# Closer steps for the last head pair, later ones for the others, and a first tile that loads x into idle buffers

## Chip, cores and metric

The kernel runs on one core of one Trainium2 chip. The metric is the device time of one execution in microseconds, as the median of several runs.

## The reference

The kernel computes two decoder layers on one sequence of 512 tokens with 1024 features, in float32. What matters here is the attention mixer of the first layer; the rest of the program follows it on the same engines.

```
n    = rms_norm(x, attn_norm)
proj = n @ w_in                                    # 12 heads, all q, k and v at once
qa, ka, va, qb, kb, vb = split(proj)               # q and k are normalized per head
oa = dilated_mixture_attention(qa, ka, va)         # 8 heads: three dilated windows, mixed by their lse
ob = differential_attention(qb, kb, vb)            # 4 heads: softmax(q1 k1) - lam * softmax(q2 k2)
ob = rms_norm(ob, b_sub_norm) * (1 - lam_init)
h  = x + concat(oa, ob) @ w_out
h  = h + conv_ffn(rms_norm(h))                     # then a recurrent mixer and a second conv_ffn
```

## The kernel before

Every matrix is kept as a sum of two halves in the matmul type, hi and lo, and a product is three matmuls: hi times hi, hi times lo, lo times hi. ScalarE (ACT) makes the hi half with a copy, VectorE (DVE) the lo half with a subtraction. That holds for weights (`split`: wh at L110, wl at L112), for x (`x_split`: xh at L237, xl at L239), and for every result that goes into a further product.

The attention stage is a list of steps, `line`, whose order for TensorE (PE) is written out by hand. Its first 128 steps are groups: 8 pairs of heads (n = 0 to 7; pairs 0 to 3 are differential heads, pairs 4 to 7 dilated ones) times 4 weight units u times 4 token blocks b. A group is 6 matmuls with 384 columns. After them come 28 fill groups, `early_out`, of 3 matmuls with 512 columns each: they begin the out projection for four output chunks with the pairs that are done. The last four fill groups use pair 6.

The attention of a pair runs between the groups of the next pairs. `place(g, f)` hangs a function f behind the step at place g; a projection group counts 1, a fill group 0.65. Matmuls and transposes are kept in this order, and other engines are scheduled from the data they need and their place in the program. With end = 16 n + 15, pair n has these functions:

- `qk_square` and `qk_norm`: squares of q and k, and their normalization, on ACT and DVE. `qk_transpose` (qkt, L418): eight transposes, then qh on ACT (L421) and ql on DVE (L423).
- `sc`: scores of rows 0 and 1, then row 2, then row 3 (`products`, two PSUM banks S, L448), each followed by `softmax_row`: maximum on DVE (L459), exp on ACT (L462), reciprocal on DVE (L463). Pairs of dilated heads then scale on ACT (L516), differential heads combine the two maps on DVE (L560).
- `tr`: transposes of one row (L469, PSUM bank pt), copied to pth on ACT (L472) and to ptl on DVE (L473). Row i takes i + 1 transposes. Dilated heads have two such steps per row, s = 0 and 1.
- `out`: the product with v (bank O, L483 to L492). Dilated heads have two, and go on with t (L531, ACT), o (L532, DVE), oh (L535, ACT) and ol (L536, DVE). Differential heads square the result and allocate the bank of its mean, obms.
- `norm` (differential heads): two matmuls for the mean into obms, Ln and Exp on ACT, six DVE operations (L586 to L590, L593).

All these PSUM banks (S, pt, qkt, O, obms) come from one pool of four, `pa`. The projection groups and `early_out` use another pool of four.

The first tile, `first_tile`, loads x and the weights of pair 0 in four units each. Both use the pool `rawp` of four buffers, so the third x unit has to wait until the first buffers are free. Squares of x (L246) and their running sum xacc (L251) stand ahead of the other work of their unit. `token_stats` turns the sum into the scale of each token in group 13 (n = 0, u = 3, b = `TOK` = 1), and the evacuation of pair 0's PSUM banks begins behind it.

At the very end, `down` adds each of the 8 output chunks to the residual (L737) and stores it (L740), from SyncE's queue.

Of the kernel before, what the change touches and what calls it, by code (L numbers as in the profile page):

```python
# [19 lines left out]
P = 128  # L20
# [8 lines left out]

ORDER = (4, 5, 6, 7, 0, 1, 2, 3)  # L30

QK_LAG = 9
AT_LAG = 12
LAST_QK_LAG = 7.5
LAST_AT_LAG = 10

OUT_GROUP = 0.65

BATCHES = ((0, 1), (2,), (3,))

SC_AT = (0, 2, 4)
TR_AT = (6.5, 8.7, 10.9, 13.1)
OUT_AT = 15
NORM_AT = 17
TOK = 1
EARLY = 4
V_BUFS = 3
WARM = 8
# [20 lines left out]
def trunk(  # L69
# [30 lines left out]
    def nm(s):  # L100
        uid[0] += 1
        return f"{s}{uid[0]}"
# [19 lines left out]
    def wunit(ap, n=1024):  # L122
        return split(load(ap, n), n)
# [101 lines left out]
    with ExitStack() as actx:  # L225
# [77 lines left out]

        def first_tile():

            units = []
            for u in range(4):
                ap = w_att[ORDER[0], u]
                if u:
                    xr = load(xT[u])  # L310
                    x_split(xr, (2 * u, 2 * u + 1))
                    units.append(wunit(ap, 2 * CW))
                    with tc.high_priority():
                        x_square(xr, (2 * u, 2 * u + 1))
                    continue
                xr = rawp.tile([P, 2 * S], F32, tag="raw", name=nm("raw"))
                wr = rawp.tile([P, 2 * CW], F32, tag="raw", name=nm("raw"))
                wh = whp.tile([P, 2 * CW], F32R, tag="wh", name=nm("wh"))
                wl = wlp.tile([P, 2 * CW], F32R, tag="wl", name=nm("wl"))
                for j in range(2):  # L320
                    cx, cw = slice(j * S, (j + 1) * S), slice(j * CW, (j + 1) * CW)
                    nc.sync.dma_start(xr[:, cx], xT[u][:, cx])
                    nc.sync.dma_start(wr[:, cw], ap[:, cw])
                    last = x_split(xr, (j,))
                    with tc.issue_after(last.ins):
                        last = A.copy(wh[:, cw], wr[:, cw])
                    V.tensor_tensor(wl[:, cw], wr[:, cw], wh[:, cw].bitcast(F32), ALU.subtract)
                units.append((wh, wl))
                with tc.issue_after(last.ins):
                    x_square(xr, (0, 1))  # L330
            nc.sync.dma_start(pt[:, KC:], par[:, KC:])
            return units

        def group(n, u, b):

            t = tiles[n]
            if b == 0:
                if u == 0:
                    t["banks"] = [mm.tile([P, S], F32, tag="mm", name=nm("pj")) for _ in range(NB)]
                if n == 0:  # L340
                    if u == 0:
                        t["units"] = first_tile()
                    t["w"] = t["units"][u]
                    prefetch(min(u, 2))
                else:
                    t["w"] = next_unit()
            if n == 0 and u == 3 and b == TOK:
                with tc.high_priority():
                    token_stats(x_acc[0])
            wh, wl = t["w"]  # L350
            tb = slice(b * P, (b + 1) * P)
            o = t["banks"][b][:, :CW]
            for j in range(2):
                k = 2 * u + j
                cw = slice(j * CW, (j + 1) * CW)
                pe(T.matmul(o, xs[k][0][:, tb], wh[:, cw], start=k == 0, stop=False))  # L356
                pe(T.matmul(o, xs[k][1][:, tb], wh[:, cw], start=False, stop=False))  # L357
                pe(T.matmul(o, xs[k][0][:, tb], wl[:, cw], start=False, stop=k == KC - 1))  # L358
            if u == 3 and n == 0:
                if b == 0:  # L360
                    t["vraw"] = smp.tile([P, S], F32, tag="t", name=nm("vraw"), bufs=1)
                with tc.high_priority():
                    A.copy(t["vraw"][:, tb], t["banks"][b][:, 2 * P : CW])
            if u == 3 and (n or b >= TOK):
                with tc.high_priority():
                    for e in range(b + 1) if n == 0 and b == TOK else (b,):
                        evacuate(n, e)

        def evacuate(n, b):

            t = tiles[n]
            p = ORDER[n]
# [4 lines left out]
            v4 = t["v"][:, b].rearrange("p (x y e) -> p x y e", x=2, y=2)  # L377
            vh, vl = (v4[:, :, 0], v4[:, :, 1]) if p < 4 else (v4[:, 0], v4[:, 1])
            pj = t["banks"][b]
            A.copy(t["raw"][:, b].rearrange("p i e -> p (i e)"), pj[:, : 2 * P])  # L380
            r = rstd[:, b : b + 1]
            vv = pj[:, 2 * P : 3 * P]
            if n == 0:

                vv = t["vraw"][:, b * P : (b + 1) * P]
            vv = vv.rearrange("p (s e) -> p s e", s=2)
            A.activation(vh, vv, AF.Copy, scale=r)
            setup_mark[0] = V.scalar_tensor_tensor(vl, vv, r, vh.bitcast(F32), ALU.mult, ALU.subtract)

        def qk_square(n, half):  # L390

# [32 lines left out]
                res.append((hi, lo))  # L424

        oT = {}

        def head_bias(h):
            bt = ap2.tile([P, S], F32, tag="bias", name=nm("bias"))
# [74 lines left out]
        def attn_a(n):  # L504

            p = ORDER[n]
            st = {}

            def sc(blocks):
                if blocks[0] == 0:  # L510
                    st["b"] = [head_bias(2 * p + s) for s in range(2)]
                rows = products(tiles[n]["qk"], blocks)
                for i in blocks:
                    for s in range(2):
                        e, r = softmax_row(rows[s, i], i, st["b"][s])
                        A.activation(e, e, AF.Copy, scale=r)  # L516
                        st["e", s, i] = e

            def tr(s, i):
                if i == 0:  # L520
                    st["pt", s] = pt_tiles()
                transposed(st["e", s, i], i, *st["pt", s])

            def out(s):
                ps = bank("O")
                pv(ps, tiles[n]["v"], *st["pt", s], s)
                if s == 0:
# [10 lines left out]
            steps = [(g, partial(sc, b)) for g, b in zip(SC_AT, BATCHES)]  # L538
            steps += [(g + s, partial(tr, s, i)) for i, g in enumerate(TR_AT) for s in range(2)]
            return steps + [(OUT_AT + s, partial(out, s)) for s in range(2)]  # L540

        def attn_b(n):

# [48 lines left out]
                A.copy(hi, o)  # L592
                V.tensor_tensor(lo, o, hi.bitcast(F32), ALU.subtract)  # L593

            steps = [(g, partial(sc, b)) for g, b in zip(SC_AT, BATCHES)]
            steps += [(g, partial(tr, i)) for i, g in enumerate(TR_AT)]
            return steps + [(OUT_AT, out), (NORM_AT, norm)]


        early = []  # L600
# [35 lines left out]
                small_setup()  # L636
                lru.extend(softplus_setup())

        place(16, setup)
        for n in range(NT):  # L640
            last = n == NT - 1
            end = 16 * n + 15
            place(end - 2, partial(urgent, qk_square, n, 0))
            place(end, partial(urgent, qk_square, n, 1))
            place(end + 0.1, partial(urgent, qk_norm, n))
            place(end + (LAST_QK_LAG if last else QK_LAG), partial(qk_transpose, n))
            for g, f in (attn_a if ORDER[n] < 4 else attn_b)(n):
                place(end + (LAST_AT_LAG if last else AT_LAG) + g, f)
        for g in range(max(len(line), max(at) + 1)):
            if g < len(line):  # L650
                line[g]()
# [59 lines left out]
    def ffn(l, nxt, last):  # L711
# [22 lines left out]
        def down(grp, acts):  # L734
            for m in range(KC):
                ps = job(acts)
                V.tensor_tensor(h[m], ps, h[m], ALU.add)  # L737
                if grp == 2:
                    if last:
                        nc.sync.dma_start(outT[m * P : (m + 1) * P, :], h[m])  # L740
                    else:
                        norm_chunk(m, nxt)

        a0 = up(0)
        a1 = up(1)
# [229 lines left out]
```

## Time and profile before

| what | value |
|---|---|
| median of 3 runs | 1200.01 us (1199.91 to 1200.17) |
| profiled execution | 1198.04 us, of which 1196.3 us are the span of the profile |
| PE busy | 1181.7 us, 99% |
| DVE busy | 811.2 us, 68% |
| ACT busy | 585.7 us, 49% |
| granted TensorE clock | 1.0 throughout |
| mean DMA rate | 96 GB/s |

The span runs from the first to the last instruction of the program. PE is busy nearly all the time, so a stretch in which it is not is what a change of order can win. Busy shares hide one thing: matmuls overlap, and a matmul that starts late shows as idle time only from the end of the one before.

### The profile page before, as it was taken

How to read it: one execution, taken by the hardware profiler on the slowest of the kernel's cores; microseconds unless marked ns; L12 is line 12 of the kernel's file. 1: busy time of each engine (PE TensorE's matmuls, PEld its weight loads, DVE VectorE, ACT ScalarE, POOL GpSimd, SP SyncE). 2: the span in 40 equal slices, each digit the busy share in tenths (PEclk: the TensorE clock that was granted, in tenths of full speed). 3: DMA queues.
4: the chain of work that ended last, by engine and by line, in shares of the span. 5: the costliest groups of instructions: out<-in, count | busy, mean ns of one | idle time of the engine just before them, and what ended most of it. 6: DMA issues, size and time to landing. Idle time of an engine off the chain costs nothing.

```text
span 1196.3 us, 14626 instructions
## 1 busy us (share of the span) xinstructions
PE 1181.7 (99%) x5566; PEld 988.7 (83%) x5566; DVE 811.2 (68%) x1326; ACT 585.7 (49%) x951; POOL 0.7 (0%) x6
## 2 busy tenths in 40 slices
PE   9999999899999999999999999999999999999998
PEld 8988888688888888888888878888888888888887
DVE  7878888587777773577446888758777763677431
ACT  7667778665444432344224688444444441444220
POOL 0000000000000000000000000000000000000000
PEclk9999999999999999999999999999999999999999
DMA  8212122063333333332333313322233233323321
GB/s 260 80 62 67 54 67 71 19 199 100 96 98 95 99 94 100 96 99 94 100 94 103 121 36 121 102 95 94 100 93 101 93 101 95 100 92 102 93 84 53
DMA packets 33766, 114.31 MB, mean 96 GB/s; under 512 B 3872, under 2 KB 4384, under 8 KB 33696
## 3 DMA queue, kind: packets, MB, share of 16 engines
q1 hardware_dynamic: 33552, 113.37, 29.7%
q8 instruction: 44, 0.72, 0.2%
q14 instruction: 26, 0.21, 0.1%
q10 hardware_dynamic: 144, 0.00, 0.0%
HBM read 111.27 MB, written 2.10 MB: 95 GB/s over the span
## 4 chain that ended last, share of the span: by engine, by line
PE 83%; ACT 4%; DVE 3%; issue 0%; ACTq 0%
PE mm L126 26%; PE mm L128 26%; PE mm L127 26%; PE pj L356 1%; PE pj L357 1%; PE pj L358 1%; ACT sm L462 1%; PE pt L469 1%; ACT sm L516 0%; ACT wh L110 0%; PE S L448 0%; DVE sm L459 0%; DVE wl L112 0%; DVE u L863 0%; PE O L490 0%
## 5 line engine op out<-in xcount | busy, mean ns | idle before, releaser
L110 ACT CAST wh<-raw 128x1024 fp32r<-128x1024 f32 (+1 forms) x207 | 211.1, 1021 | 291.6 <-PE mm L127 256.9
L128 PE MATMUL mm<-xh,wl 128*128 128x512 f32 x896 | 348.6, 389 | 0.0
L127 PE MATMUL mm<-xl,wh 128*128 128x512 f32 x896 | 348.6, 389 | 0.0
L126 PE MATMUL mm<-xh,wh 128*128 128x512 f32 x896 | 348.6, 389 | 0.0
L112 DVE TENSOR_TENSOR wl<-raw,wh 128x1024 fp32r<-128x1024 f32 (+1 forms) x207 | 244.7, 1183 | 45.6 <-ACT wh L110 42.8
L127 PEld LDWEIGHTS mm<-xl,wh 128*128 128x128 f32 x896 | 168.2, 188 | 35.2
L126 PEld LDWEIGHTS mm<-xh,wh 128*128 128x128 f32 x896 | 168.2, 188 | 35.0
L128 PEld LDWEIGHTS mm<-xh,wl 128*128 128x128 f32 x896 | 168.2, 188 | 34.8
L707 DVE SCALAR_TENSOR_TENSOR cv<-us,pt,cv 128x511 f32<-128x511 f32 (+2 forms) x216 | 160.4, 747 | 3.5
L126 PE MATMUL mm<-fh,wh 128*128 128x512 f32 x384 | 149.4, 389 | 0.0
L127 PE MATMUL mm<-fl,wh 128*128 128x512 f32 x384 | 149.4, 389 | 0.0
L128 PE MATMUL mm<-fh,wl 128*128 128x512 f32 x384 | 149.4, 389 | 0.0
L703 DVE TENSOR_TENSOR us<-mm,rs 128x512 f32<-128x512 f32 x104 | 71.6, 688 | 93.9 <-PE mm L128 93.7
L737 DVE TENSOR_TENSOR h<-mm,h 128x512 f32<-128x512 f32 x48 | 33.2, 691 | 141.4 <-PE mm L128 141.4
L356 PE MATMUL pj<-wh,xh 128*128 128x384 f32 x256 | 91.9, 359 | 0.9 <-ACT wh L110 0.6
L728 ACT CAST fh<-cv 128x512 fp32r<-128x512 f32 x48 | 29.8, 621 | 126.4 <-DVE cv L725 126.4
L358 PE MATMUL pj<-wl,xh 128*128 128x384 f32 x256 | 86.8, 339 | 0.7 <-DVE wl L112 0.7
L357 PE MATMUL pj<-wh,xl 128*128 128x384 f32 x256 | 86.3, 337 | 0.0
L705 ACT ACTIVATE cv<-us,pt 128x512 f32<-128x512 f32 x104 | 84.2, 813 | 0.8 <-DVE us L703 0.6
L126 PEld LDWEIGHTS mm<-fh,wh 128*128 128x128 f32 x384 | 72.1, 188 | 15.1
L127 PEld LDWEIGHTS mm<-fl,wh 128*128 128x128 f32 x384 | 72.1, 188 | 14.9
L128 PEld LDWEIGHTS mm<-fh,wl 128*128 128x128 f32 x384 | 72.1, 188 | 14.9
(202 smaller groups left out, 1234.1 us busy)
## 6 DMA issues: line engine op xcount, KB each, us to landing
raw<-in_w_up_dram SPq DMA_DIRECT2D x96, 512.0 KB, 3.5
raw<-in_w_dn_dram SPq DMA_DIRECT2D x48, 512.0 KB, 3.5
raw<-in_w_att_dram SPq DMA_DIRECT2D x31, 384.0 KB, 3.2
raw<-in_w_ri_dram SPq DMA_DIRECT2D x16, 512.0 KB, 3.5
raw<-in_w_ao_dram SPq DMA_DIRECT2D x8, 512.0 KB, 4.0
raw<-in_w_ro_dram SPq DMA_DIRECT2D x8, 512.0 KB, 3.5
raw<-in_xT_dram SPq DMA_DIRECT2D x7, 512.0 KB, 4.4
out_dram<-h SPq DMA_DIRECT2D x8, 256.0 KB, 2.0
```

Source lines behind the costliest of these rows:

```text
L110: A.copy(hi, src)
L112: V.tensor_tensor(lo, src, hi.bitcast(F32), ALU.subtract)
L126: order(T.matmul(out, wh, xh, start=first, stop=False))
L127: order(T.matmul(out, wh, xl, start=False, stop=False))
L128: return order(T.matmul(out, wl, xh, start=False, stop=last))
L356: pe(T.matmul(o, xs[k][0][:, tb], wh[:, cw], start=k == 0, stop=False))
L357: pe(T.matmul(o, xs[k][1][:, tb], wh[:, cw], start=False, stop=False))
L358: pe(T.matmul(o, xs[k][0][:, tb], wl[:, cw], start=False, stop=k == KC - 1))
L703: V.tensor_tensor(u, ps, state["rs"], ALU.mult)
L705: A.activation(c, u, AF.Identity, scale=col(wcol + (taps - 1) * stride), bias=col(bcol))
L707: V.scalar_tensor_tensor(c[:, d:], u[:, : S - d], col(wcol + (taps - 1 - d) * stride), c[:, d:], ALU.mult, ALU.add)
L737: V.tensor_tensor(h[m], ps, h[m], ALU.add)
```

## The change

The four parts are independent of each other in the code.

- Places. The constants become two tables, `PLACES` for pairs 0 to 6 and `LAST` for pair 7. For pairs 0 to 6, in groups behind the end of the pair: score steps stay at 12, 14 and 16. The transposes of rows 0 and 3 stay in their group, those of rows 1 and 2 go one group later (for the dilated pairs some steps of s = 1 too). The output goes from 27 to 28, where it stands directly ahead of the next pair's first scores, and the normalization from 29 to 30.5, where it stands behind the next pair's second scores. For pair 7 the three score steps, the transposes and the outputs move together: scores behind fill groups 14, 15 and 16 of 28 (counted from 1) instead of 14, 17 and 20; transposes behind 18 to 23 instead of 24 to the end; both outputs behind 24 instead of behind all 28. Pair 6's later steps run among the fill groups as well: its last transposes and its outputs go one or two fill groups later.
- First tile. x goes into the buffers of pth and ptl, which are not used before pair 0's transposes. All ten loads of x and weights are issued at once, then the rest of the parameters. The squares of a unit come behind the splits of the next one, without priority.
- Token statistics go from group 13 to group 17; evacuation of pair 0 no longer waits for them. The scaling of pair 0's v, its `qk_norm` and the small setup (four more loads, L263 to L267) follow there.
- The last output chunk is added in two halves, and each half is stored as soon as it is there, the second one from ACT's queue.

```diff
-QK_LAG = 9
-AT_LAG = 12
-LAST_QK_LAG = 7.5
-LAST_AT_LAG = 10
+BATCHES = ((0, 1), (2,), (3,))
+PLACES = dict(qk=9, sc=(12, 14, 16), tr=(18.9, 21.1, 23.7, 25.8), step=1, out=28, norm=30.5)
+LAST = dict(qk=7.5, sc=(9.8, 10.5, 11.2), tr=(12.7, 13.4, 14.2, 15), step=0.35, out=16.2, norm=18)
 OUT_GROUP = 0.65
-BATCHES = ((0, 1), (2,), (3,))
-SC_AT = (0, 2, 4)
-TR_AT = (6.5, 8.7, 10.9, 13.1)
-OUT_AT = 15
-NORM_AT = 17
-TOK = 1
+TOK = 17
...
         def first_tile():
+            xr = [ap2.tile([P, 13 * P], F32, tag=("pth", "ptl")[u % 2], name=nm("xr"))[:, : 2 * S] for u in range(4)]
+            wr = [rawp.tile([P, 2 * CW], F32, tag="raw", name=nm("raw")) for u in range(4)]
+            for u in range(4):
+                for j in range(2 if u == 0 else 1):
+                    cx, cw = (slice(j * S, (j + 1) * S), slice(j * CW, (j + 1) * CW)) if u == 0 else (slice(None),) * 2
+                    nc.sync.dma_start(xr[u][:, cx], xT[u][:, cx])
+                    nc.sync.dma_start(wr[u][:, cw], w_att[ORDER[0], u][:, cw])
+            nc.sync.dma_start(pt[:, KC:], par[:, KC:])
             units = []
             for u in range(4):
-                ap = w_att[ORDER[0], u]
                 if u:
-                    xr = load(xT[u])
-                    x_split(xr, (2 * u, 2 * u + 1))
-                    units.append(wunit(ap, 2 * CW))
-                    with tc.high_priority():
-                        x_square(xr, (2 * u, 2 * u + 1))
+                    x_split(xr[u], (2 * u, 2 * u + 1))
+                    units.append(split(wr[u], 2 * CW))
+                    x_square(xr[u - 1], (2 * u - 2, 2 * u - 1))
                     continue
...
-                with tc.issue_after(last.ins):
-                    x_square(xr, (0, 1))
-            nc.sync.dma_start(pt[:, KC:], par[:, KC:])
+            x_square(xr[3], (6, 7))
             return units
...
-            if n == 0 and u == 3 and b == TOK:
-                with tc.high_priority():
-                    token_stats(x_acc[0])
...
+        def first_stats():
+            token_stats(x_acc[0])
+            for b in range(NB):
+                scale_v(0, b, tiles[0]["vraw"][:, b * P : (b + 1) * P])
...
+        def where(n):
+            return LAST if n == NT - 1 else PLACES
...
-            steps += [(g + s, partial(tr, s, i)) for i, g in enumerate(TR_AT) for s in range(2)]
-            return steps + [(OUT_AT + s, partial(out, s)) for s in range(2)]
+            steps += [(g + s * at["step"], partial(tr, s, i)) for i, g in enumerate(at["tr"]) for s in range(2)]
+            return steps + [(at["out"] + s * at["step"], partial(out, s)) for s in range(2)]
...
-        place(16, setup)
+        place(TOK, partial(urgent, first_stats))
+        place(TOK + 1, setup)
         for n in range(NT):
-            last = n == NT - 1
             end = 16 * n + 15
             place(end - 2, partial(urgent, qk_square, n, 0))
             place(end, partial(urgent, qk_square, n, 1))
-            place(end + 0.1, partial(urgent, qk_norm, n))
-            place(end + (LAST_QK_LAG if last else QK_LAG), partial(qk_transpose, n))
+            place(end + 0.1 if n else TOK + 0.1, partial(urgent, qk_norm, n))
+            place(end + where(n)["qk"], partial(qk_transpose, n))
...
                 ps = job(acts)
-                V.tensor_tensor(h[m], ps, h[m], ALU.add)
-                if grp == 2:
-                    if last:
-                        nc.sync.dma_start(outT[m * P : (m + 1) * P, :], h[m])
-                    else:
-                        norm_chunk(m, nxt)
+                for t in (slice(0, S // 2), slice(S // 2, S)) if last and grp == 2 and m == KC - 1 else (slice(0, S),):
+                    V.tensor_tensor(h[m][:, t], ps[:, t], h[m][:, t], ALU.add)
+                    if last and grp == 2:
+                        (A if t.start else nc.sync).dma_start(outT[m * P : (m + 1) * P, t], h[m][:, t])
+                if grp == 2 and not last:
+                    norm_chunk(m, nxt)
```

## Rows read from the trace of the kernel before

**Rows 1.** Windows: busy us (instructions) of each engine, clock, DMA share, GB/s.

```profile
60.00:240.00 180.00, 172.77 (x1048) 149.29 (x1047) 138.87 (x398) 132.92 (x342) 0.00 (x0) 1.00 0.18 56
...
240.00:1192.00 952.00, 951.15 (x4191) 785.91 (x4190) 623.02 (x782) 412.10 (x517) 0.00 (x0) 1.00 0.31 98
```

**Rows 2.** Waits of PE, 60 to 246 us: total us, times, longest.

```profile
PE mm L126 <- ACT oh L535: 2.0, 1, 2.0
PE pt L469 <- DVE sm L560: 1.5, 3, 0.5
PE pt L469 <- DVE ptl L473: 1.4, 2, 0.7
PE pt L469 <- DVE mx L459: 1.0, 1, 1.0
PE O L484 <- DVE ptl L473: 0.5, 2, 0.2
PE O L492 <- DVE ptl L473: 0.5, 2, 0.2
PE O L490 <- ACT pth L472: 0.2, 1, 0.2
```

**Rows 3.** Timeline of the first tile: start us, us, instruction, [idle before, releaser].

```profile
8.31 1.34 ACT L237 ACTIVATE xh<-raw,pt 128x512 fp32r<-128x512 f32 x2 [0.65 <-DMA raw<-in_xT_dram]
9.07 1.42 DVE L239 SCALAR_TENSOR_TENSOR xl<-raw,pt,xh 128x512 fp32r<-128x512 f32 x2 [0.69 <-ACT xh L237]
...
10.34 0.33 PE L357 MATMUL pj<-wh,xl 128*128 128x384 f32 x1
...
10.51 0.34 PE L358 MATMUL pj<-wl,xh 128*128 128x384 f32 x1
10.60 0.82 ACT L110 CAST wh<-raw 128x768 fp32r<-128x768 f32 x1
...
11.47 0.44 PE L356 MATMUL pj<-wh,xh 128*128 128x384 f32 x1 [0.62 <-ACT wh L110]
...
11.75 0.34 PE L357 MATMUL pj<-wh,xl 128*128 128x384 f32 x1
11.80 0.95 DVE L112 TENSOR_TENSOR wl<-raw,wh 128x768 fp32r<-128x768 f32 x1
```

**Rows 4.** DMA issues: count, size of each, us from issue to landing.

```profile
out_dram<-h SPq DMA_DIRECT2D x8, 256.0 KB, 2.0
...
pt<-in_par_dram SPq DMA_DIRECT2D x1, 238.5 KB, 6.3
```

**Rows 5.** Timeline of the token statistics and pair 0's normalization, DVE and PE.

```profile
23.89 0.15 DVE L291 TENSOR_SCALAR ssq<-tok 128x4 f32<-128x4 f32 x1
...
31.03 1.28 DVE L409 TENSOR_TENSOR qkraw<-qkraw,rsy 128x512 f32<-128x512 f32 x2
...
35.61 1.03 PE L418 MATMUL qkt<-ident,qkraw 128*128 128x128 f32 x8
```

**Rows 6.** Timeline of pair 3's scores and transposes, PE and DVE.

```profile
122.04 0.50 PE L448 MATMUL S<-qh,qh 64*128 64x512 f32 x2
...
124.39 0.68 DVE L587 SCALAR_TENSOR_TENSOR obt<-obms,obt 128x512 f32<-128x512 f32 x1
...
133.01 0.74 DVE L560 SCALAR_TENSOR_TENSOR sm<-sm,sum,sm 128x512 f32<-128x512 f32 x1
...
134.77 0.60 PE L469 MATMUL pt<-ident,sm 128*128 128x128 f32 x4
```

**Rows 7.** Timeline of ACT in the last pair: first exp, last output.

```profile
216.33 0.40 ACT L462 ACTIVATE sm<-sm,mx 128x128 f32<-128x128 f32 x1 [1.33 <-DVE mx L459]
...
237.16 0.58 ACT L531 COPY t<-O 64x512 f32<-64x512 f32 x1 [0.67 <-PE O L490]
...
238.50 0.62 ACT L535 CAST oh<-o 128x512 fp32r<-128x512 f32 x1 [0.76 <-DVE o L532]
```

**Rows 8.** Window of the last pair, from its first scores to the wait.

```profile
214.90:239.00 24.10, 21.49 (x123) 16.16 (x122) 12.97 (x39) 15.27 (x40) 0.00 (x0) 1.00 0.00 1
```

More of the change, by code (lines that the diff above doesn't have):

```diff
@@ L304, in first_tile @@
         def first_tile():
+            xr = [ap2.tile([P, 13 * P], F32, tag=("pth", "ptl")[u % 2], name=nm("xr"))[:, : 2 * S] for u in range(4)]
[6 more added lines that the diff above has]
+            nc.sync.dma_start(pt[:, KC:], par[:, KC:])
             units = []
             for u in range(4):
-                ap = w_att[ORDER[0], u]
                 if u:
-                    xr = load(xT[u])
-                    x_split(xr, (2 * u, 2 * u + 1))
-                    units.append(wunit(ap, 2 * CW))
-                    with tc.high_priority():
-                        x_square(xr, (2 * u, 2 * u + 1))
+                    x_split(xr[u], (2 * u, 2 * u + 1))
+                    units.append(split(wr[u], 2 * CW))
+                    x_square(xr[u - 1], (2 * u - 2, 2 * u - 1))
                     continue
-                xr = rawp.tile([P, 2 * S], F32, tag="raw", name=nm("raw"))
-                wr = rawp.tile([P, 2 * CW], F32, tag="raw", name=nm("raw"))
                 wh = whp.tile([P, 2 * CW], F32R, tag="wh", name=nm("wh"))
@@ L320, in first_tile @@
                 for j in range(2):
[L321 to L324, printed above, removed]
+                    cw = slice(j * CW, (j + 1) * CW)
+                    last = x_split(xr[0], (j,))
                     with tc.issue_after(last.ins):
-                        last = A.copy(wh[:, cw], wr[:, cw])
-                    V.tensor_tensor(wl[:, cw], wr[:, cw], wh[:, cw].bitcast(F32), ALU.subtract)
+                        A.copy(wh[:, cw], wr[0][:, cw])
+                    V.tensor_tensor(wl[:, cw], wr[0][:, cw], wh[:, cw].bitcast(F32), ALU.subtract)
                 units.append((wh, wl))
-                with tc.issue_after(last.ins):
-                    x_square(xr, (0, 1))
-            nc.sync.dma_start(pt[:, KC:], par[:, KC:])
+            x_square(xr[3], (6, 7))
             return units
@@ L358, in group @@
                 pe(T.matmul(o, xs[k][0][:, tb], wl[:, cw], start=False, stop=k == KC - 1))
-            if u == 3 and n == 0:
-                if b == 0:
-                    t["vraw"] = smp.tile([P, S], F32, tag="t", name=nm("vraw"), bufs=1)
+            if u == 3:
                 with tc.high_priority():
[L363 to L367, printed above, removed]
+                    evacuate(n, b)
+                    if n:
+                        scale_v(n, b, t["banks"][b][:, 2 * P : CW])
         def evacuate(n, b):
             t = tiles[n]
-            p = ORDER[n]
             if b == 0:
@@ L375, in evacuate, with scale_v @@
                 t["v"] = ap2.tile([P, NB, 2 * P], F32R, tag="v", name=nm("v"), bufs=V_BUFS)
-            v4 = t["v"][:, b].rearrange("p (x y e) -> p x y e", x=2, y=2)
-            vh, vl = (v4[:, :, 0], v4[:, :, 1]) if p < 4 else (v4[:, 0], v4[:, 1])
+                if n == 0:
+                    t["vraw"] = smp.tile([P, S], F32, tag="t", name=nm("vraw"), bufs=1)
             pj = t["banks"][b]
             A.copy(t["raw"][:, b].rearrange("p i e -> p (i e)"), pj[:, : 2 * P])
+            if n == 0:
+                A.copy(t["vraw"][:, b * P : (b + 1) * P], pj[:, 2 * P : CW])
+        def scale_v(n, b, v):
+            t = tiles[n]
+            v4 = t["v"][:, b].rearrange("p (x y e) -> p x y e", x=2, y=2)
+            vh, vl = (v4[:, :, 0], v4[:, :, 1]) if ORDER[n] < 4 else (v4[:, 0], v4[:, 1])
             r = rstd[:, b : b + 1]
[L382 to L386, printed above, removed]
+            vv = v.rearrange("p (s e) -> p s e", s=2)
             A.activation(vh, vv, AF.Copy, scale=r)
             setup_mark[0] = V.scalar_tensor_tensor(vl, vv, r, vh.bitcast(F32), ALU.mult, ALU.subtract)
+        def first_stats():
+            token_stats(x_acc[0])
+            for b in range(NB):
+                scale_v(0, b, tiles[0]["vraw"][:, b * P : (b + 1) * P])
         def qk_square(n, half):
@@ L536, in out @@
                     V.tensor_tensor(lo, st["o"], hi.bitcast(F32), ALU.subtract)
-            steps = [(g, partial(sc, b)) for g, b in zip(SC_AT, BATCHES)]
-            steps += [(g + s, partial(tr, s, i)) for i, g in enumerate(TR_AT) for s in range(2)]
-            return steps + [(OUT_AT + s, partial(out, s)) for s in range(2)]
+            at = where(n)
+            steps = [(g, partial(sc, b)) for g, b in zip(at["sc"], BATCHES)]
+            steps += [(g + s * at["step"], partial(tr, s, i)) for i, g in enumerate(at["tr"]) for s in range(2)]
+            return steps + [(at["out"] + s * at["step"], partial(out, s)) for s in range(2)]
         def attn_b(n):
@@ L593, in norm @@
                 V.tensor_tensor(lo, o, hi.bitcast(F32), ALU.subtract)
-            steps = [(g, partial(sc, b)) for g, b in zip(SC_AT, BATCHES)]
-            steps += [(g, partial(tr, i)) for i, g in enumerate(TR_AT)]
-            return steps + [(OUT_AT, out), (NORM_AT, norm)]
+            at = where(n)
+            steps = [(g, partial(sc, b)) for g, b in zip(at["sc"], BATCHES)]
+            steps += [(g, partial(tr, i)) for i, g in enumerate(at["tr"])]
+            return steps + [(at["out"], out), (at["norm"], norm)]
         early = []
@@ L644, in trunk @@
             place(end, partial(urgent, qk_square, n, 1))
-            place(end + 0.1, partial(urgent, qk_norm, n))
-            place(end + (LAST_QK_LAG if last else QK_LAG), partial(qk_transpose, n))
+            place(end + 0.1 if n else TOK + 0.1, partial(urgent, qk_norm, n))
+            place(end + where(n)["qk"], partial(qk_transpose, n))
             for g, f in (attn_a if ORDER[n] < 4 else attn_b)(n):
-                place(end + (LAST_AT_LAG if last else AT_LAG) + g, f)
+                place(end + g, f)
         for g in range(max(len(line), max(at) + 1)):
```

## The prediction

> **What bounds the kernel now.** Read first the windows by stage: from 240 us on TensorE (PE) is busy 951.15 of 952 us, so nothing there can be won but the last store; between 60 and 240 it stands idle 7.2 of 180 us [rows 1]. The change must earn its time in the first 240 us, and it earns it only where PE waits. So read next the waits of PE: after 60 us they are few, and each names the row that came last [rows 2]. Then the timeline at the start, where the second x unit comes late [rows 3].
>
> An idle time reads short. Matmuls overlap: one of 0.33 us is followed by the next after 0.17 us (10.34, 10.51), so an idle of 0.62 us ahead of 11.47 is a distance of 0.96 us where 0.17 is normal, a loss of 0.79 [rows 3]. I add 0.16 us to each idle time below. Three waits on L560 then cost 2.0 us, two on L473 ahead of transposes 1.7, one on L459 1.2, the two at L484 0.8, the two at L492 0.8, the one at L490 0.4, the one on L535 2.2 [rows 2]. With 1.7 us at the start (below) that is about 10.8 us, the most that can come back apart from small change.
>
> **The change part by part.** Durations are from the profiled execution: span 1196.3 us, 1198.04 us with what lies around it. The median of the runs shown is 1200.01 us; I take the same saving off it.
>
> *Start.* Before, PE lost 0.79 us at 11.47, and 0.89 us more until its third matmul: wl ended at 12.75, where 11.47 + 0.28 + 0.17 = 11.92 would have been due, and the handover adds 0.06 [rows 3]. On ScalarE (ACT) two squares stood between xh and wh: xh ends at 9.65, wh could run 0.82 us to 10.47 and PE was free at 10.68. That first wait goes. On VectorE (DVE) the xacc additions stood between xl (ends 10.49) and wl: wl now ends at 10.49 + 0.95 = 11.44, and the third matmul is due at 10.68 + 0.35 = 11.03, so 0.46 us stays. Saving 1.7 - 0.46 = 1.2 us. The x units no longer wait for a weight buffer; that itself is worth little at unit 1, whose x came in the first batch anyhow. Its landing is the unknown: more loads now follow it at once. Before, xh waited 0.65 us for it until 8.31, and the 238.5 KB of parameters that followed took 6.3 us to land, as if they had queued behind the units [rows 3, 4]; if five units instead share the engines evenly, x could come 2 us later. Bounds -0.8 to +1.7. The parameters and the four loads of the small setup go further back on SP's queue; their first reader is the bias of the first scores, after group 27, some 10 us later than any of them should land. POOL has nothing here.
>
> The token statistics move from group 13 to the end of group 17, and the first q/k normalization behind them. Before, 8.4 us passed from the first DVE step at 23.89 to the end of that normalization at 32.31; the transposes that need it came at 35.61 [rows 5]. Group 17 ended seven groups of 1.04 us ahead of those, at 28.3. Now the first step comes at about 28.3 - 1.2 + 0.3 for the handover = 27.4, the transposes at 34.4: 7.0 us. The chain itself is short (small operations, and 1.28 us for the two halves), the 8.4 were mostly other work in between, so I take a wait of 0.3; bounds 0 and 1.5. Behind the waiting transposes stand all projection matmuls. Saving of the start: 0.9.
>
> *Pairs 0 to 6, places.* A group is 6 matmuls, 1.04 us. The third row of pairs 1 to 3 moves one group later, more than the 0.67 us that each waits: 2.0 us back. Their outputs move a group as well: the 0.8 us at L484 goes. Pair 4 lost 0.9 us (of the two L473 waits) and 1.2 us (L459) one behind the other; one group of delay takes 1.04 off the sum: 1.0, bounds 1.0 and 2.1. Output and next scores now follow without a group between, as do scores and normalization: two switches fewer for four pairs; the first matmul after a break hands over after 0.28 us, not 0.17 (11.47, 11.75) [rows 3], 0.1 us for each of eight switches. 0.7, bounds 0 and 1.4.
>
> Against it: the fourth row's place stays in the same group, and PE comes there 0.67 us earlier. In pair 3 its row was ready at 133.01 + 0.74 = 133.75 and PE came at 134.77 [rows 6]: 1.0 us of slack becomes 0.35. The normalization (six DVE operations; if all take the 0.68 us of L587, some 4 us) now falls later into the same DVE burst. Ahead of the row it takes up to 1.2 us, behind it nothing. I take 0.3 us for each of three pairs, 0.9; bounds 0 and 2.6 (three times 1.2 - 0.35). Sum for pairs 0 to 5: 2.0 + 0.8 + 1.0 + 0.7 - 0.9 = 3.6; bounds 1.2 and 6.3.
>
> Pair 6: the second L473 wait (0.8) and one L492 wait (0.4). The transposes move one fill group (0.68 us) later, but so does the second row whose evacuation they wait for: 0.4, bounds -0.3 and 1.2.
>
> *Last pair.* Before, all fill groups were used up when the transposes of the last two rows and both outputs ran; then t, o and oh came one after the other, from 237.16 to 239.12, and PE stood [rows 7]. Now the outputs stand after fill group 24 of 28, and four fill groups (12 matmuls of 512 columns; at 0.17 us for 384 [rows 3] 0.23 us each, 2.7 us) follow: they cover the 2.2 us. That part is firm. The other waits of the stretch (L492 0.4, L490 0.4) add 0.8, so 3.0 us can come back, less the new waits.
>
> New waits: from 214.9 to 239 ACT is busy 15.27 us [rows 8], 1.7 of it t and oh after the outputs, so 13.6 us belong ahead of them. The first exp stood 1.3 us behind the first scores [rows 7], so the last copy ends 14.9 us after them at the earliest, with no gap on ACT, and DVE's half, of the size of L587's 0.68 us [rows 6], 0.7 us later. PE needs 24.1 - 3.4 us of waits (this stretch's and pair 6's L492) - 2.7 fill = 18.0 us to the end of the second output, so the first (2560 columns each, 1.2 us) is due 15.6 us after the first scores; it needs all but the last copy (0.6 like oh [rows 7]), 14.9 - 0.6 + 0.7 = 15.0. ACT may stand 0.6 us, and stood 8.8 of 24.1 us before. I take 1.1 us of new waits, nearer the gapless end, since the scores of all rows now lie ready early; bounds 0 and 3.9 (half of the old idle time stays). Saving 1.9, bounds -0.9 and 3.0.
>
> *Last store.* The 256 KB store takes 2.0 us to landing [rows 4]. Two half additions end a little later than one whole; the second store moves half the bytes and leaves from ACT, which has nothing behind it. Saving 0.2, bounds -0.1 and 0.4. The Trainium skill, page "Perfetto Trace Analysis", section "DMA Optimizations", says that transfers below 2 KB carry much overhead each; the halves have rows of 1 KB. By that the saving would be 0 and the sum 0.2 smaller; no run here shows it.
>
> Sum: 0.9 + 3.6 + 0.4 + 1.9 + 0.2 = 7.0 us: span 1189.3, profiled 1191.0, median 1200.01 - 7.0 = **1193.0 us**.
>
> **Rivals.** *Every wait goes and none comes.* 1.7 + 6.3 + 1.2 + 3.0 + 0.4 = 12.6 us, 1187.4. For it: all delays exceed the waits. Against: ACT gapless for 14 us.
>
> *The waits come back one step later.* In pairs 1 to 4 and the last, ACT and DVE are the late ones (L560, L459, L473) [rows 2]; a later third row only shifts the wait to the fourth row or the output, and the last pair starves. Left: the start, the switches and the store, 0.9 + 0.7 + 0.2 = 1.8 us, 1198.2. For it: fourth rows with 0.35 us left. Against: transposes of row 4 did not wait in pairs 1 to 3. The same Trainium skill page, section "Optimization Strategy", says that a gap repeating on the engine that should be busy can mean too little PSUM for the next tile; by that rule the gap would stay, and this rival's 1198.2 would be the time. The trace agrees for pair 4 (L459 and L473 free a bank), not for pairs 1 to 3, where data (L560) came last.
>
> *Slower: a bank held by the normalization.* Output allocates the bank of the mean, and the normalization now comes behind the next pair's second scores. If the third scores need that bank, they wait for L587: ahead of pair 3 it ended at 125.07 where the scores came at 122.04 [rows 6], 3.0 us, plus 1.2 for the later place: 4.2 us in four pairs, 16.8 - 7.0 = 9.8 slower, 1209.8. It decides from 1.8 us per pair (7.0 / 4). Against: before, too, L587 came after those scores and they did not wait; two other banks served.
>
> **Chances.** Forecast 0.74 (its own range 1188.0 to 1197.0), every wait gone 0.10, waits come back 0.11, slower 0.05. The range 1188.0 to 1198.3 leaves out the first and the last rival. 0.2% is 2.4 us, about what a measurement can tell from no change: faster 0.84, same 0.11, slower 0.05.
>
> **What would show it.** Right: PE's waits on L560 gone; no wait on oh ahead of the out projection; the wait ahead of the second x unit on wl alone, near 0.3 us idle; ACT almost without idle time through the last pair. Wrong: waits at qkt near 35 us, at the fourth row's transposes, at S products, or a late xh at 8.3 us. PE idle between 60 and 240 us should fall from 7.2 to about 2.5 us.

## The result, and the profile after

The changed kernel is slower: 1208.28 us (median of 4 runs, 1206.37 to 1209.08) against 1199.96 us (4 runs, 1199.04 to 1200.17), ratio 1.0069, 95% interval 1.0051 to 1.0086. The forecast of 1193.0 us (1188.0 to 1198.3) did not hold. The profiled execution took 1208.45 us; its span is 1206.4 us, 10.1 more than before.

Three matmuls cut each trace into four stages: the first transposition of q and k of pair 0 (qkt), the last pair's first scores (S of 128 columns), and the first matmul of the normalization that follows the attention (nrm). Their starts give, in us:

```
                                  to qkt   to S    to nrm  to the end
before                            35.61   179.39   54.77   926.53
after                             35.58   192.49   51.85   926.48
forecast of the change            -0.9     -4.0    -1.9     -0.2
measured                           0.0    +13.1    -2.9     -0.05
```

The last pair gave more than forecast, the start nothing in this execution, and the pairs in between lost 13.1 us. The windows before and behind the attention say the same. From 250 us PE is as busy as it was [rows 1]; between 60 and 250 it is idle 15.0 us, and its mean clock is 0.96:

```profile
60.00:250.00 190.00, 175.03 (x1045) 155.59 (x1044) 140.21 (x398) 133.98 (x342) 0.00 (x0) 0.96 0.17 54
250.00:1202.00 952.00, 951.20 (x4192) 786.27 (x4192) 623.16 (x782) 412.10 (x517) 0.00 (x0) 1.00 0.31 98
```

The waits of PE in the changed kernel, 60 to 260 us (total us, times, longest):

```profile
PE pt L467 <- DVE sm L559: 12.2, 3, 4.2
PE pt L467 <- DVE mx L457: 1.3, 1, 1.3
PE pt L467 <- DVE o L530: 1.1, 1, 1.1
PE pt L467 <- DVE ptl L471: 0.4, 1, 0.4
```

Most rows of [rows 2] are gone: the outputs' waits, the wait on oh, one of the two on ptl. The wait of transposes on the combined row (L560 before, L559 now) still counts three, but they have grown from 1.5 to 12.2 us and have moved from the third row to the fourth. The timeline of PE shows one of them, in pair 3: the scores of the fourth row at 99.97, the transposition of q and k, then the wait, and behind it projections 0.33 to 0.46 us apart where 0.17 was normal:

```profile
99.97 0.50 PE L446 MATMUL S<-qh,qh 64*128 64x512 f32 x2
...
111.06 1.03 PE L413 MATMUL qkt<-ident,qkraw 128*128 128x128 f32 x8
...
116.25 1.11 PE L467 MATMUL pt<-ident,sm 128*128 128x128 f32 x4 [4.15 <-DVE sm L559]
117.02 0.67 PE L347 MATMUL pj<-wh,xh 128*128 128x384 f32 x1
117.48 0.52 PE L348 MATMUL pj<-wh,xl 128*128 128x384 f32 x1
117.81 0.52 PE L349 MATMUL pj<-wl,xh 128*128 128x384 f32 x1
```

Windows over that stretch (busy us of PE, granted clock, DMA share, GB/s). The wait is paid twice: behind an idle time of 4.15 us PE runs at 0.50, the lower of its two levels (1.2 of 2.4 GHz), from 116.2 until about 120.7; these 4.5 us at half the clock are some 2.2 us lost:

```profile
107.00:111.90 4.90, 4.90 (x34) 1.00 0.25 80
111.90:116.20 4.30, 0.20 (x2) 0.76 0.53 151
116.20:117.00 0.80, 0.75 (x4) 0.50 0.44 173
117.00:120.70 3.70, 3.70 (x14) 0.50 0.00 0
120.70:125.00 4.30, 4.30 (x33) 0.97 0.02 5
```

Why the combined row came so late stands in the timeline of DVE. A row has two halves, one for each of the pair's two score maps, and each half takes a maximum over its scores (L457) before the exponential and the combination (L559):

```profile
103.61 0.67 DVE L457 CUSTOM_DVE_ANT_0 sm<-S,bias 128x512 f32<-128x512 f32 x1
...
109.05 0.68 DVE L588 TENSOR_TENSOR oby<-oby,obt 128x512 f32<-128x512 f32 x1
...
109.99 0.74 DVE L589 SCALAR_TENSOR_TENSOR ob<-ob,pt,oby 128x512 f32<-128x512 f32 x1
...
111.52 0.68 DVE L592 TENSOR_TENSOR ol<-ob,oh 128x512 fp32r<-128x512 f32 x1
112.12 0.68 DVE L457 CUSTOM_DVE_ANT_0 sm<-S,bias 128x512 f32<-128x512 f32 x1
...
115.46 0.74 DVE L559 SCALAR_TENSOR_TENSOR sm<-sm,sum,sm 128x512 f32<-128x512 f32 x1
```

Both halves' scores were there before 101. The first maximum runs at 103.61, the second only at 112.12, behind the last steps of the normalization (L585 to L592; L589, the last read of y, ends at 110.73), though DVE did many other things in between.

The start, ACT and PE. A square of x (L240) now stands ahead of the first xh, which starts at 4.09; the second half of the weights is copied when it lands, at 6.68. The x of unit 1 comes no earlier than before: its xh starts at 8.26 behind a wait of 0.53 us for the landing (8.31 and 0.65 before), the late xh that the prediction had named as a sign of being wrong. No matmul of unit 1 waits any more [rows 3], but in unit 0 PE waits ahead of 5.25 and 7.25:

```profile
3.55 0.63 ACT L240 ACTIVATE xsq<-xr 128x512 f32<-128x512 f32 x1 [1.53 <-DMA xr<-in_xT_dram]
4.09 0.71 ACT L231 ACTIVATE xh<-xr,pt 128x512 fp32r<-128x512 f32 x1
...
6.68 0.51 ACT L322 CAST wh<-raw 128x384 fp32r<-128x384 f32 x1 [0.87 <-DMA raw<-in_w_att_dram]
...
8.26 1.33 ACT L231 ACTIVATE xh<-xr,pt 128x512 fp32r<-128x512 f32 x2 [0.53 <-DMA xr<-in_xT_dram]
```

```profile
5.25 0.44 PE L347 MATMUL pj<-wh,xh 128*128 128x384 f32 x1 [0.38 <-ACT wh L322]
...
7.25 0.44 PE L347 MATMUL pj<-wh,xh 128*128 128x384 f32 x1 [0.70 <-ACT wh L322]
```

and then runs without a gap at half the clock (windows of PE):

```profile
8.50:11.60 3.10, 3.10 (x11) 0.50 1.02 410
11.60:14.00 2.40, 2.40 (x15) 0.97 1.03 395
```

In the last pair ACT shows no idle time from 231 to 242 us, and then waits for PE as in [rows 7]; the wait on oh is covered by the four fill groups, and one new wait stands (PE ahead of 239.69, for the bank of pair 6's first output, which L530 is the last to read):

```profile
238.95 0.68 DVE L530 TENSOR_TENSOR o<-O,t 64x512 f32<-64x512 f32 x1 [1.67 <-ACT t L529]
```

```profile
239.69 0.65 PE L467 MATMUL pt<-ident,sm 128*128 128x128 f32 x4 [1.09 <-DVE o L530]
```

The stores (DMA issues, to set beside [rows 4]): a half takes nearly as long as a whole.

```profile
out_dram<-h SPq DMA_DIRECT2D x7, 256.0 KB, 2.0
...
out_dram<-h SPq DMA_DIRECT2D x1, 128.0 KB, 1.7
out_dram<-h ACTq DMA_DIRECT2D x1, 128.0 KB, 1.8
```

### The profile page after: what moved, and what is told of

Same layout as the page of the kernel before. It is cut to its first block, busy times and chain, and to the rows that moved or that the text cites. A ratio compares the mean times of both kernels' runs of the same rounds, so it can differ in the third digit from the quotient of the medians.

```text
span 1206.4 us, 14631 instructions
## 1 busy us (share of the span) xinstructions
PE 1184.7 (98%) x5566; PEld 996.9 (83%) x5566; DVE 812.9 (67%) x1327; ACT 586.7 (49%) x951; POOL 0.7 (0%) x6
## 4 chain that ended last, share of the span: by engine, by line
PE 89%; DVE 5%; ACT 5%; issue 0%; DMA 0%; SPq 0%; DVEq 0%
PE mm L121 26%; PE mm L120 26%; PE mm L122 26%; PE pj L347 3%; PE pj L349 3%; PE pj L348 2%; ACT sm L460 1%; PE pt L467 1%; DVE wl L106 1%; PE S L446 1%; ACT sm L514 0%; DVE sm L457 0%; DVE qkraw L404 0%; DMA raw<-in_w_att_dram 0%; PE qkt L413 0%
## 5 line engine op out<-in xcount | busy, mean ns | idle before, releaser
L739 DVE TENSOR_TENSOR h<-mm,h 128x512 f32<-128x512 f32 (+1 forms) x49 | 33.2, 680 | 141.4 <-PE mm L122 141.4
L348 PE MATMUL pj<-wh,xl 128*128 128x384 f32 x256 | 89.0, 348 | 0.0
```

Source lines behind the costliest of these rows:

```text
L739: V.tensor_tensor(h[m][:, t], ps[:, t], h[m][:, t], ALU.add)
```

## The experiments

**Theory A.** The pool of the rows has two buffers with the tag "sm3", and four things of a pair take them in turn: the square obsq that feeds the mean, y (the scale made from the mean, which L589 reads last), and the two e tiles of the next pair's fourth row (row 3), one for each half:

```python
sq = smp.tile([P, S], F32, tag="sm3", name=nm("obsq"))
y = smp.tile([P, S], F32, tag="sm3", name=nm("oby"))
e = smp.tile([P, n], F32, tag=f"sm{i}", name=nm("sm"))
```

The first e takes the buffer of obsq, the second that of y, and its maximum can't start before L589 has ended. The change moves the normalization 1.5 groups towards the next pair's third scores, which stay where they were. **Theory B**: no buffer, DVE just has the normalization's work ahead in its order. **Theory C**: the later rows and outputs, or another part, make the waits.

*y in an idle buffer (e_buf).*

```diff
-                y = smp.tile([P, S], F32, tag="sm3", name=nm("oby"))
+                y = ap2.tile([P, 13 * P], F32, tag="pth", name=nm("oby"))[:, :S]
```

> The changed kernel with one edit: the copy y that the normalization makes of its bank lies in the idle buffer of the high transposed products (tag pth) and no longer in one of the two buffers (tag sm3) that the row maxima's e tiles use. Theory A (the second half of row 3 waits for a sm3 buffer that y holds until the normalization's last read): the three PE waits of 4.1 to 4.4 us at the fourth row's transposes in pairs 1 to 3 shrink to under 1 us each, the granted clock no longer falls behind them, pj105 starts some 13 us earlier than in the changed kernel, and the time is 1190 to 1196 us. Theory B (VectorE simply has the normalization's work ahead of row 3's in its order, whatever the buffer): the three waits stay at 2 us or more, and the time stays at 1204 to 1209 us.

1191.81 us (1191.13 to 1193.56) against 1198.57, ratio 0.9938 (0.9923 to 0.9954). The waits on L559 are gone; five short ones for the bank that ptl reads are left, and the clock is 1.00 from 60 to 160 us:

```profile
PE pt L467 <- DVE ptl L471: 3.3, 5, 0.9
PE pt L467 <- DVE o L530: 1.1, 1, 1.1
```

In DVE's timeline of the same pair both maxima (96.42, 97.85) now stand ahead of y's last steps:

```profile
96.42 0.68 DVE L457 CUSTOM_DVE_ANT_0 sm<-S,bias 128x512 f32<-128x512 f32 x1
...
97.85 0.67 DVE L457 CUSTOM_DVE_ANT_0 sm<-S,bias 128x512 f32<-128x512 f32 x1
...
101.85 0.68 DVE L588 TENSOR_TENSOR oby<-oby,obt 128x512 f32<-128x512 f32 x1
103.66 0.74 DVE L589 SCALAR_TENSOR_TENSOR ob<-ob,pt,oby 128x512 f32<-128x512 f32 x1
104.32 0.74 DVE L559 SCALAR_TENSOR_TENSOR sm<-sm,sum,sm 128x512 f32<-128x512 f32 x1
```

The edit moves y and nothing else, and it brings the maxima ahead, so A holds against B.

*The normalization earlier (e_norm29).*

```diff
-PLACES = dict(qk=9, sc=(12, 14, 16), tr=(18.9, 21.1, 23.7, 25.8), step=1, out=28, norm=30.5)
+PLACES = dict(qk=9, sc=(12, 14, 16), tr=(18.9, 21.1, 23.7, 25.8), step=1, out=28, norm=29)
```

> The changed kernel with the normalization of the regular pairs at place 29 instead of 30.5; rows and outputs stay at their new places. Theories A and B (the normalization, by its buffer or by its place in VectorE's order, holds back the second half of row 3): its last read comes ahead of row 3, the three waits of 4.1 to 4.4 us go, and the time is 1190 to 1196 us. Theory C (the later places of rows and outputs make the waits by themselves, or the new places of the last pair and the first tile do): the waits stay, 1204 to 1209 us.

1195.09 us, ratio 0.9970 (0.9959 to 0.9981). C falls as the main cause: rows and outputs are late, yet the time is below that of before. I had expected the waits to go; they only shrank:

```profile
PE pt L467 <- DVE sm L559: 4.2, 3, 1.4
```

y is still read last (L589 at 103.03) ahead of the second maximum (105.78): less late, the same order.

*The normalization behind the next scores (e_norm32).*

```diff
-PLACES = dict(qk=9, sc=(12, 14, 16), tr=(18.9, 21.1, 23.7, 25.8), step=1, out=28, norm=30.5)
+PLACES = dict(qk=9, sc=(12, 14, 16), tr=(18.9, 21.1, 23.7, 25.8), step=1, out=28, norm=32.5)
```

> The changed kernel with the normalization at place 32.5 instead of 30.5, which is behind the next pair's third scores (place 32 on this scale); y stays in the shared sm3 buffers, and now row 3's e tiles stand ahead of it for them. Theory A (the shared buffer, by its order): the second half of row 3 no longer waits for y, the three waits of 4.1 to 4.4 us at the fourth row's transposes go, and the time is 1190.5 to 1195 us, though the normalization is later than in any kernel so far. Theory C, that a later normalization is what costs, wherever it stands: waits of 4 us or more, 1208 us or more.

1190.04 us, ratio 0.9936 (0.9923 to 0.9950). With one constant and no other buffer the waits on L559 are gone, although the normalization is later than in any kernel so far: its last read, at 108.85, holds nobody up. What counts is who takes the buffer first.

```profile
PE O L482 <- DVE ptl L471: 2.0, 3, 0.9
PE pt L467 <- DVE o L530: 1.1, 1, 1.1
PE pt L467 <- DVE ptl L471: 0.3, 1, 0.3
```

*The later normalization alone, in the kernel before (e_only_norm).*

```diff
-NORM_AT = 17
+NORM_AT = 18.5
```

> The kernel before with the normalization alone 1.5 places later (18.5 instead of 17 behind the lag), nothing else changed. Theory A: the fourth row's scores of the second half of row 3 now wait for the buffer that y holds, with less room than in the changed kernel, since the rows' places stay early: a wait of 3 us or more appears at the fourth row's transposes of pairs 1 to 3, and the time is 1208 to 1217 us. Theory C (the later rows and outputs are needed for the waits): no new wait, 1199 to 1201 us.

1212.65 us, ratio 1.0106 (1.0088 to 1.0125): this one constant costs more than the whole change (some 15 us between qkt and S; 13.1 in the changed kernel, whose other parts gave something back).

```profile
PE pt L469 <- DVE sm L560: 10.1, 3, 3.4
```

*The buffer in the kernel before (e_pre_buf).*

```diff
-                y = smp.tile([P, S], F32, tag="sm3", name=nm("oby"))
+                y = ap2.tile([P, 13 * P], F32, tag="pth", name=nm("oby"))[:, :S]
```

> The kernel before with y of the normalization in the pth buffer and nothing else changed. If the shared buffer costs only where the normalization comes too late for row 3 (the places of before leave 1.0 us of room at the fourth row): the time of the kernel before, 1198 to 1200 us, within 0.2 percent. If it cost something in the kernel before too (a part of the third rows' waits): 1196 to 1198 us, faster by over 0.2 percent.

1199.30 us, ratio 1.0003 (0.9994 to 1.0012): no change. The same order stood in the trace of before, with L590 ending at 128.16 and the second maximum behind it, but the row was ready 1.0 us before PE came [rows 6]:

```profile
127.42 0.74 DVE L590 SCALAR_TENSOR_TENSOR ob<-ob,pt,oby 128x512 f32<-128x512 f32 x1
128.31 0.69 DVE L459 CUSTOM_DVE_ANT_0 sm<-S,bias 128x512 f32<-128x512 f32 x1
```

**The other parts.** *The first tile and the later token statistics alone (e_start).*

```diff
-PLACES = dict(qk=9, sc=(12, 14, 16), tr=(18.9, 21.1, 23.7, 25.8), step=1, out=28, norm=30.5)
-LAST = dict(qk=7.5, sc=(9.8, 10.5, 11.2), tr=(12.7, 13.4, 14.2, 15), step=0.35, out=16.2, norm=18)
+PLACES = dict(qk=9, sc=(12, 14, 16), tr=(18.5, 20.7, 22.9, 25.1), step=1, out=27, norm=29)
+LAST = dict(qk=7.5, sc=(10, 12, 14), tr=(16.5, 18.7, 20.9, 23.1), step=1, out=25, norm=27)
...
-                for t in (slice(0, S // 2), slice(S // 2, S)) if last and grp == 2 and m == KC - 1 else (slice(0, S),):
+                for t in (slice(0, S // 2), slice(S // 2, S)) if False else (slice(0, S),):
```

> The changed kernel with all places of rows, outputs, normalization and of the last pair put back to those of before and the last store whole: what is left is the first tile that loads x into idle buffers and the later token statistics. My reading of the trace of the changed kernel (the waits at unit 1 go, but an idle of 1.11 us and a stretch at half the clock take their place): 1199.5 to 1200.5 us, no change. Rival, the term of the forecast (0.9 us gained at the start): 1198.8 to 1199.3 us.

1198.64 us (1195.89 to 1200.13) against 1198.57: ratio 0.9994 (0.9985 to 1.0003). Both ranges were set against a kernel before of 1200; against the one beside it, no change that stands out from the noise. The interval does not rule out the forecast's 0.9 us either (ratio 0.9992).

*The old first tile in e_buf (e_oldstart), and the new one with its first squares held back (e_sq).* e_oldstart puts first_tile() of the kernel before in place of the new one:

```diff
...
-                    x_split(xr[u], (2 * u, 2 * u + 1))
-                    units.append(split(wr[u], 2 * CW))
-                    x_square(xr[u - 1], (2 * u - 2, 2 * u - 1))
+                    xr = load(xT[u])
+                    x_split(xr, (2 * u, 2 * u + 1))
+                    units.append(wunit(ap, 2 * CW))
+                    with tc.high_priority():
+                        x_square(xr, (2 * u, 2 * u + 1))
...
```

and e_sq is e_buf with

```diff
...
-                        A.copy(wh[:, cw], wr[0][:, cw])
+                        held = A.copy(wh[:, cw], wr[0][:, cw])
...
+                with tc.issue_after(held.ins):
+                    x_square(xr[0], (0, 1))
```

> The version with y in the pth buffer (1191.8 us), with the first tile of the kernel before put back (x through the four staging buffers, squares of x with priority); the later token statistics, the places and the halved store stay. Reading 1, that the new first tile gives nothing on average (its gain is eaten by later landings and an idle at the second half of unit 0): 1191.3 to 1192.5 us, the same. Reading 2, the term of the forecast (0.9 us of waits at unit 1 that go): 1192.5 to 1193.3 us.

> The version with y in the pth buffer (1191.8 us), with the squares of x's first unit held behind that unit's two weight copies on ScalarE, as in the kernel before. If the square that stands ahead of the first scaled copy of x delays the start (0.4 us at the first xh) and with it brings the stretch at half the clock: the first projection starts at 4.88 us instead of 5.25, no stretch at half the clock, and the time is 0.4 to 1.8 us lower, 1190.0 to 1191.4 us. If the landing of the second half of w0 (6.2 to 7.4 us in the runs so far) sets the first unit's end: the earlier start only makes the wait for that half longer, and the time is the same, 1191.5 to 1192.3 us.

1192.08 us (1191.58 to 1192.25) and 1191.32 us (1189.60 to 1193.00). By these times the new first tile is worth 0.3 us (1192.08 - 1191.81) or, with the squares held back, 0.8, both less than the runs scatter; and the order of the squares is not shown to matter: in e_sq the first xh starts at 3.67, but the second weight copy still waits for its landing (6.21), and half the clock is there too (0.63 from 8.5 to 11.6 us).

*The last pair's old places in e_buf (e_oldlast).*

```diff
-LAST = dict(qk=7.5, sc=(9.8, 10.5, 11.2), tr=(12.7, 13.4, 14.2, 15), step=0.35, out=16.2, norm=18)
+LAST = dict(qk=7.5, sc=(10, 12, 14), tr=(16.5, 18.7, 20.9, 23.1), step=1, out=25, norm=27)
```

> The version with y in the pth buffer (1191.8 us), with the last pair's places put back to those of the kernel before. The trace's reading (the stretch from the last pair's first scores to the next stage's first matmul is 2.9 us shorter in every kernel with the dense places): 1194.3 to 1195.0 us. The forecast's term for the last pair (1.9 us): 1193.5 to 1194.0 us. If the dense places give nothing by themselves and the gain is that of the other pairs: 1191.5 to 1192.3 us.

1195.00 us, 3.2 more than e_buf: the dense places are worth that, and the wait of 2.0 us on oh is back.

*The fourth row a group later, without and with the outputs (e_tr4, e_tr4_out), on e_sq.*

```diff
-PLACES = dict(qk=9, sc=(12, 14, 16), tr=(18.9, 21.1, 23.7, 25.8), step=1, out=28, norm=30.5)
+PLACES = dict(qk=9, sc=(12, 14, 16), tr=(18.9, 21.1, 23.7, 26.2), step=1, out=28, norm=30.5)
```

```diff
-PLACES = dict(qk=9, sc=(12, 14, 16), tr=(18.9, 21.1, 23.7, 25.8), step=1, out=28, norm=30.5)
+PLACES = dict(qk=9, sc=(12, 14, 16), tr=(18.9, 21.1, 23.7, 26.2), step=1, out=29, norm=30.5)
```

> The version with y in the pth buffer and the first squares behind the splits (1191.3 us), with the fourth row's transposes of the regular pairs one group later (26.2 instead of 25.8), so that a projection group stands between the transposes of q and k and them. Five waits of 0.6 to 0.9 us on the bank that ptl reads (3.2 us in all) should shrink: 1188.0 to 1190.0 us. If the outputs (still at 28) then wait for the fourth row's ptl, the gain is given back: 1190.5 to 1192 us.

> As the run with the fourth row one group later, and the outputs one group later too (29 instead of 28). The waits of 3.2 us shrink and the outputs find ptl ready: 1188.0 to 1190.0 us. If the later outputs hold pth (and with it y and the next pair's rows) too long: 1191 us or more.

1189.63 us, ratio 0.9927 (0.9915 to 0.9939), the lowest median, though not apart from e_norm32 (1190.04): of the waits on ptl 1.0 us is left at the transposes, and 1.1 us of waits of the outputs came. And 1205.62 us, ratio 1.0062 (1.0050 to 1.0074). The outputs a group later, with the normalization where it was, bring a wait of another kind: the mean's matmul now stands 1.5 groups behind the output it is taken from, and waits for the square's rounded copy (obh) in all four pairs. I had expected a hold on pth.

```profile
PE obms L129 <- ACT obh L126: 8.3, 4, 3.0
PE obms L130 <- DVE obl L127: 1.6, 4, 0.5
```

*Both remedies (e_both)*, e_tr4 with y back in its shared buffer and the normalization behind:

```diff
-PLACES = dict(qk=9, sc=(12, 14, 16), tr=(18.9, 21.1, 23.7, 26.2), step=1, out=28, norm=30.5)
+PLACES = dict(qk=9, sc=(12, 14, 16), tr=(18.9, 21.1, 23.7, 26.2), step=1, out=28, norm=32.5)
...
-                y = ap2.tile([P, 13 * P], F32, tag="pth", name=nm("oby"))[:, :S]
+                y = smp.tile([P, S], F32, tag="sm3", name=nm("oby"))
```

> The changed kernel with the normalization at 32.5 (y in the shared sm3 buffers), the fourth row one group later (26.2) and the squares of x's first unit behind its splits: the two best versions (1190.0 and 1189.6 us) in one. If the waits that each removes are different ones (on L559 and on the bank that ptl reads): 1188.0 to 1189.5 us. If the fourth row, now later, meets the later normalization on VectorE or holds the outputs at 28: 1190 us or more.

1190.47 us (1189.51 to 1192.54), ratio 0.9931 (0.9918 to 0.9945): not apart from either. Three waits of the output for the fourth row's ptl (2.5 us) took the place of those removed.

## Why the prediction was wrong

The step that failed is "Against it", in the pairs' places: it charged the later normalization 0.3 us for each of three pairs, 0.9, "bounds 0 and 2.6". That bound counted the DVE time that could fall ahead of the row, by 1.2 us that no row gives (1.5 groups are 1.6 us). It left out that the second half of the row may not begin before the normalization's last read, since both use one buffer. Measured, each of the three pairs lost 4.1 to 4.3 us at the fourth row (idle 3.9 to 4.15, and the 0.16 that an idle time reads short), and then 1.6 to 2.2 us at half the clock, a cost for which the sum had no term: moving y alone shortens the stretch from qkt to S by 16.5 us (192.49 - 176.02).

- *The pairs' other terms* were nearly right as a sum: 4.0 us forecast for pairs 0 to 6, with the 0.9 of "Against it" taken off, and 3.4 in e_buf (179.39 - 176.02), without the buffer. Waits of 0.65 to 0.78 us remain there at the fourth row of three pairs, 2.7 us with 0.16 added to each, just above the bound of 2.6; but they are for the bank that ptl reads, not for the row. A wait of 0.9 us for such a bank stands at the third row of pair 4.
- *The rival "a bank held by the normalization"* had the right holder, the right sign and nearly the time (1209.8), and got 0.05; it named a PSUM bank and the third scores. The near time is luck: it counted 4.2 us in four pairs, where three pairs waited and the half clock came on top. The scores did not wait; the maximum behind them did. My argument against it, that the same order had stood before without a wait, was true of the bank and said nothing of the SBUF buffer, which had 1.0 us of room. *"The waits come back one step later"* named the fourth row, but only as a gain lost.
- *The Trainium skill*, page "Perfetto Trace Analysis", section "Optimization Strategy", says that a gap repeating on the engine that should be full can mean too little SBUF or PSUM for the next tile. I had weighed it for PSUM alone. The three gaps on L559 (3.9 to 4.15 us) agree with its SBUF half: they go when one tile gets another buffer (e_buf).
- *Start*, forecast 0.9: in the profiles qkt of pair 0 starts at 35.61, 36.04, 36.08 and about 36.1 with the old first tile, mean 36.0, and at 33.94 to 36.35 in ten kernels with the new one, mean 35.0. So 1.0 us is there on average, but the times show 0 (e_start), 0.3 or 0.8 us (e_oldstart beside e_buf and e_sq). In three of the profiles with the new first tile and no stretch at half the clock (e_buf, e_tr4_out, e_both) the one wait of unit 1 is the forecast one, on wl, 0.36 to 0.37 us. Whether the term holds for the time stays open. The token statistics cost no wait.
- *Last pair*, forecast 1.9: measured 2.9 here and 3.2 in e_oldlast. The new waits were 1.1 us by idle time, the size assumed (1.1), but at another place: ACT, without idle time, came late to t (238.34, where the output had ended at 237.76), and so the bank of pair 6's first output came free late; the last pair's own copies held nothing up. What came back was more than the 3.0 I counted, and why stays open.
- *Last store*, forecast 0.2: from the last matmul's end to the span's end 3.73 us, where 3.81 were before, and 3.78 in e_buf; 0.1 or less.

In e_buf start, pairs, last pair and store are -1.0, -3.4, -2.9 and 0.0: 7.2 us of the span, where the sum of the forecast was 7.0; by the medians it is 6.8 (1198.57 - 1191.81). What was missing is the wait for the buffer, with the half clock behind it. That the other terms add up so closely is in part luck: the pairs gave 0.6 less and the last pair 1.0 more than forecast, and the start of this execution is one of the early ones.

## What to carry to other kernels

Before a step is moved, list who else takes turns in the buffers that it holds, in the order of the code, and find the last reader of each: here the wait for a buffer stood in the trace under the name of the late data, not of the buffer. Room at such a place (1.0 us here) is shared by all that stands ahead of it, and a step that is moved over the next user (30.5 to 32.5) can cost less than one moved towards it. Where slack may fall short by 3 to 4 us, count the half clock behind the wait beside the wait itself; here it added 1.6 to 2.2 us to each wait of 4.

## What the runs showed of the hardware

- Behind each of the three idle times of about 4 us the granted clock was 0.50 for 3.2 to 4.5 us, while PE was fully busy, and behind that of 3.17 us in e_only_norm for 5.7 (146.0 to 151.7); behind the three of up to 1.4 us in e_norm29 it was not (1.00 from 60 to 160 us). The length of the idle time alone does not tell: in e_tr4_out there are three of 1.76 us, and behind the one that ends at 122.16 the clock was 0.56 (122.1 to 126.0), behind the other two 1.00.
- At the start the new first tile met projections 0.32 us apart in 6 of 10 profiles, with a granted clock of 0.50 to 0.63 in four of them (two rows said 1.00), and qkt came at 35.11 to 36.35; in the other four it came at 33.94 to 34.66. With the old first tile this was met in none of four. The wait ahead of it (unit 0's second half) was 0.5 to 1.4 us in the six, but 0.8 in e_norm32 and 0.9 in e_tr4_out too, which kept the clock; what decides was not found.
- A store of 128 KB took 1.7 to 1.8 us, one of 256 KB 2.0.
